# Two fetches of v earlier in a hybrid decoder layer, and two attention lanes that advance at every second step

## The chip, the cores and the metric

The kernel runs on one core of a Trainium2 chip. The metric is device time in microseconds of one execution; lower is better. TensorE (PE) does the matmuls, VectorE (DVE) and ScalarE (ACT) the elementwise work, GpSimd (POOL) a few small operations and part of the DMA issues, SyncE (SP) most of the DMA issues. Each engine works through its own queue of instructions in order.

## The reference

One layer on 256 tokens of width 2048, in float32. A normalised input is multiplied by one wide weight `w_in`, whose columns feed two mixers: chunked gated linear attention (GLA, branch a) and differential attention (branch b). Each mixer's output is normalised per head and gated, multiplied by its branch weight, and both are merged under sigmoid gates, multiplied by `w_out`, normalised and added to x.

```python
h = rmsnorm(x, pre_norm_g[l])
proj = h @ w_in[l]
(a_q, a_k, a_v, a_g, a_lr, b_q, b_k, b_v, b_g, m_a, m_b) = jnp.split(proj, offsets, axis=-1)
gk = jax.nn.log_sigmoid((a_lr @ gla_gk_w2[l] + gla_gk_b[l]).astype(jnp.float32)) / GATE_LOGIT_NORMALIZER
o_a = gla_chunked(a_q..., a_k..., a_v..., gk...)
o_a = rmsnorm(o_a, gla_norm_g[l]).reshape(B, S, GLA_VAL_DIM) * jax.nn.silu(a_g)
y_a = o_a @ w_branch_a[l]
o_b = diff_attention(b_q..., b_k..., b_v..., lam)
o_b = rmsnorm(o_b, diff_norm_g[l]) * (1.0 - lam_init)
o_b = o_b.reshape(B, S, DIFF_VAL_DIM) * jax.nn.silu(b_g)
y_b = o_b @ w_branch_b[l]
merged = jax.nn.sigmoid(m_a) * y_a + jax.nn.sigmoid(m_b) * y_b
x = x + rmsnorm(merged @ w_out[l], post_norm_g[l])
```

## The kernel before

**Products.** A float32 weight tile comes from HBM (`raw`, three buffers, loaded by SP at L308) and is split into two parts of reduced format: `hi` by ACT (L357) and the rest `lo` by DVE (L358), three buffers each. The stationary or moving operand (`xs` for the input, `oah`/`oal` for branch a's output, `obh`/`obl` for branch b's) is split in the same way, and each product is hi times hi, hi times lo, lo times hi. A weight tile has two halves; `take` splits three halves ahead of their use (AHEAD = 3). PE's matmuls for all of these stand at L552, in `mm`.

**Stages.** First the projection for v, k, q and the gates, with the blocks of `w_in` combined to save products; then the gates of branch a (`ag0` to `ag3`), m02, the last heads' q and k (`diff_heads(3)`, tiles `dq` and `dk` in column tiles of 128), m03; then `y00` to `y03` (branch a times its weight), the mixed steps of the branch (`branch_steps`: the rest of y03, parts of y10 and y11, and the products of the combined set `ys0`, whose weights are built in `part_e`, `part_b` and `part_f`), the late steps, and `w_out`.

**Tasks beside the main line.** GLA and differential attention run as generators in the list `tasks`. `pump(n)` advances the first n by one step after a piece of the main line; `pump_eager` advances, halfway through a column tile, those of the first two that last said "go". What a step issues is put in after the main line's matmuls before it. The tasks that matter here:

- `gla_scores(hf)` makes the scores of half the GLA heads (matmuls of `xq` and `xk`), hf 0 and then 1, and marks `scores0`, `scores1` when done.
- `gla_out` multiplies the scores by v. v was stored to HBM early on, in four parts (one per head) with a high and a low half each. `bring(n)` fetches part n into two tiles `vback` (512 KB each) with two DMAs on POOL's queue (L183, `fetch`). `weigh(n)` does nine matmuls of 512 columns on them (`product`, L525), two squares on ACT, the power for the norm on POOL (`rsqrt`, L459, tile `gssq`), and the gating on DVE (L1031). `turn_heads` transposes the result (L1037) into `oah`/`oal`.
- `diff_lane(0)` and `diff_lane(1)` work through the eight pairs of heads of branch b. Lane 0 starts at `scores1`, lane 1 when the fourth `weigh` is issued ("weighed"). Each fetches its q and k with small DMAs on SP's queue (`place`, L1066, into `q2`, `kh` and `kl`, after a memset of half of `kl` on POOL, L1079), makes scores (L1111 to L1117), turns them (L1142), multiplies them by v (`weighted`, L1153 to L1155; its own norm has a power on POOL, tile `de`), writes the gated head into `ogb` (L1166 on DVE), and at last turns the pair (`turned_out`, four transposes at L1172) into `obh` (ACT) and `obl` (DVE, L603).

**Buffers.** `vback`, `q2`, `kh`, `kl`, `gp`, the fetched q and k of GLA and `xs` all come from the pool `u` with 18 slots; a tile takes a free slot and its first writer waits for the slot's last reader.

The bodies that the change touches, of `gla_out` and of the branch's loop:

```python
        for n in range(7):
            if n < 4:
                weigh(n)
            if n < 2:
                bring(n + 2)
...
    for step in branch_steps():
        next(parts if step[0] in ("part", "ys0") else plain)
        if step == ("part", "ys0", 7, 1):
            merged(0, whole[0])
        pump(LANES if len(tasks) > 1 else 1)
```

LANES is 3. The branch has 26 steps in the order `.p.p.p.p.pp.pp.pp.p.p.p..p`, a dot being a step of y03, y10 or y11 (12 matmuls) and p one of ys0 (6 matmuls).

Of the kernel before, what the change touches and what calls it, by code (L numbers as in the profile page):

```python
# [24 lines left out]
LANES = 3  # L25
# [92 lines left out]
def half_set_steps(name):  # L118

    steps = []  # L120
    for prod in LATE:
        r = {1: 0, 2: 2}.get(prod)
        steps += [("part", name, prod, h) if r is None else (name, r, h) for h in range(2)]
    return steps


def branch_steps():

    plain = [("y03", r, h) for r in (2, 3) for h in range(2)]
    plain += [(f"y1{g}", r, h) for g in range(2) for r in range(2) for h in range(2)]  # L130
    parts = half_set_steps("ys0")
    return [(plain, parts)[n == "p"].pop(0) for n in BRANCH_ORDER]
# [11 lines left out]
def hybrid_kernel(ctx: ExitStack, tc, xt, xn, preg, postg, w, w2, gkb, glag, lamv, diffg, ident_d, causal_d, lmask_d, out):  # L144
# [18 lines left out]
    def u2(shape, name, dtype=F32):  # L163
        count[0] += 1
        return pools[1].tile(shape, dtype, tag="u2", name=f"{name}_{count[0]}")

    def sm(shape, name, dtype=F32, bufs=2):
        count[0] += 1
        return pools[0].tile(shape, dtype, tag=name, name=f"{name}_{count[0]}", bufs=bufs)
# [11 lines left out]
    def fetch(d, name, make, queue=pool):  # L181
        t = make(list(d.shape), name, d.dtype)
        tc.keep_in_program_order(queue.dma_start(t, d))  # L183
        return t

    def ps(tag):
        count[0] += 1
        return psum.tile([P, 512], F32, tag=tag, name=f"{tag}_{count[0]}")
# [269 lines left out]
    def rsqrt(dst, src):  # L458
        pool.tensor_tensor(out=dst, in0=src, in1=neg_half[:, : src.free_size()], op=ALU.pow)  # L459
# [41 lines left out]
    tasks = []  # L501
    ts, heads, m0 = {}, {}, []
    DONE = object()
    done = set()
# [4 lines left out]
    def advance(some):  # L509
        with tc.issue_after(latest[0]):  # L510
            for task in some:
                r = next(task, DONE)
                (eager.add if r == "go" else eager.discard)(task)
                if r is DONE:
                    tasks.remove(task)

    def pump(n=1):
        advance(tasks[:n])
# [4 lines left out]
    def product(out, pairs, first, last, **kw):  # L523
        for n, (lhs, rhs) in enumerate(pairs):
            i = pe.matmul(out, lhs, rhs, start=first and n == 0, stop=last and n == len(pairs) - 1, **kw)  # L525
        return i.ins
# [74 lines left out]
    def split_out(bank, hi, lo, gain):  # L601
        act.activation(hi, bank, AF.Copy, scale=gain)
        dve.scalar_tensor_tensor(out=lo, in0=bank, scalar=gain, in1=f32(hi), op0=ALU.mult, op1=ALU.subtract)  # L603
# [401 lines left out]
    def gla_out():  # L1005
        back = {}

        def bring(n):
            back[n] = [fetch(d, "vback", u) for d in vspill[n]]

        def weigh(n):
            hf, h = n // 2, n % 2
            if h == 0:
                for i in (2 * hf, 2 * hf + 1):
                    oah[i], oal[i] = u2([P, 2, 2, S], "oah", F32R), u2([P, 2, 2, S], "oal", F32R)
            (ah, al), (xh_, xl_) = att[hf], back.pop(n)
            banks = [ps("bg"), ps("bg")]
            trio = lambda i, b: ((ah[:, i, h, :], xh_[:, b, :]), (ah[:, i, h, :], xl_[:, b, :]), (al[:, i, h, :], xh_[:, b, :]))
            product(banks[0], trio(0, 0), True, True)
            product(banks[1], trio(2, 0), True, False)  # L1020
            product(banks[1], trio(1, 1), False, True)
            ssq = sm([P, 2], "gssq")
            junk = sm([P, 512], "junk", BF16, bufs=1)
            for b in range(2):
                act.activation(junk, banks[b], AF.Square, accum_out=ssq[:, b : b + 1])
            dve.scalar_tensor_tensor(out=ssq, in0=ssq, scalar=1.0 / 512.0, in1=gla_eps, op0=ALU.mult, op1=ALU.add)
            rsqrt(ssq, ssq)
            dve.tensor_tensor(out=ssq, in0=ssq, in1=half_rstd, op=ALU.mult)
            o = gates[n]
            for b in range(2):  # L1030
                dve.scalar_tensor_tensor(out=o[:, b, :], in0=banks[b], scalar=ssq[:, b : b + 1], in1=o[:, b, :], op0=ALU.mult, op1=ALU.mult)  # L1031

        def turn_heads(hf, j):
            bank = ps("bg")
            for h in range(2):
                for b in range(2):
                    pe.transpose(bank[:, P * (2 * h + b) : P * (2 * h + b) + P], gates[2 * hf + h][:, b, P * j : P * j + P], ident)  # L1037
            i = 2 * hf + j // 2
            hi = oah[i][:, j % 2].rearrange("p h t -> p (h t)")
            lo = oal[i][:, j % 2].rearrange("p h t -> p (h t)")  # L1040
            split_out(bank, hi, lo, glag_s[:, j : j + 1])

        while "scores0" not in done:
            yield
        bring(0)
        bring(1)
        yield
        while "scores1" not in done or len(gates) < 4:
            yield
        for n in range(7):  # L1050
            if n < 4:
                weigh(n)
            if n < 2:
                bring(n + 2)
            if n == 3:
                done.add("weighed")
            if n > 2:
                for j in range(2):
                    turn_heads((n - 3) // 2, 2 * ((n - 3) % 2) + j)
            yield "go"  # L1060
        done.add("out")

    obh, obl, ob_f32, ob_sums, values = [], [], [], {}, {}
# [175 lines left out]

    gates = []  # L1240
    tasks.append(gla_out())
    tasks.extend(diff_lane(n) for n in range(2))

# [110 lines left out]
    def merged(g, banks):  # L1354
        for b in range(2):
            t, src = gb[g][:, b, :], banks[b]
            if g < 2:
                src = ycell(b, g)
                dve.tensor_tensor(out=src, in0=banks[b], in1=src, op=ALU.add if 512 * g == BRANCH_COLS[0] else ALU.subtract)
            dve.scalar_tensor_tensor(out=t, in0=t, scalar=1.0, in1=src, op0=ALU.add, op1=ALU.mult)  # L1360
            dve.tensor_tensor(out=t, in0=t, in1=parts_a[g][:, b, :], op=ALU.add)
        tasks.append(turn(g))
# [152 lines left out]
    yc.extend(u([P, 1024], "yc") for _ in range(2))  # L1515
    parts, plain = half_set("ys0", b_ops, ob_sums, ycell, BRANCH_COLS), branch_plain(banks)
    pinned[0] = True
    for step in branch_steps():
        next(parts if step[0] in ("part", "ys0") else plain)
        if step == ("part", "ys0", 7, 1):  # L1520
            merged(0, whole[0])
        pump(LANES if len(tasks) > 1 else 1)
    pinned[0] = False
    for gen in (parts, plain):
        assert next(gen, DONE) is DONE
# [137 lines left out]
```

## Time and profile before

| what | us |
|---|---|
| time, three runs | 1095.33, 1095.60, 1097.95 (median 1095.6) |
| the profiled execution's own time | 1098.33 |
| its span, first to last instruction | 1096.5 |
| PE busy | 1081.7 |
| DVE busy | 931.6 |
| ACT busy | 721.3 |
| POOL busy | 154.2 |
| bytes read and written in HBM | 260.98 MB and 26.21 MB |

A line of the profile names an engine, a line of the kernel, an operation and the tiles `out<-in`, without their buffer numbers. "Busy" is time in which an engine executes; a busy PE can still run at a lower clock, which the column PEclk gives. The chain of work that ended last goes back from the last instruction to what released each step. In a timeline, what stands in brackets is the idle time ahead of an instruction on its engine and what ended it. Queue q0 is that of POOL's DMAs, q1 that of SP's.

### The profile page before, as it was taken

The numbers are of one execution on the slowest core, as the hardware profiler recorded it, in microseconds if no ns is written. First come the engines' busy times: TensorE is split into PE (matmuls) and PEld (weight loads), VectorE is DVE, ScalarE is ACT, GpSimd is POOL, SyncE is SP. The second block draws the span as 40 slices with busy tenths as digits, with TensorE's granted clock in tenths as the row PEclk, the third lists the DMA queues.
The fourth block names the chain that finished last, engine by engine and source line by source line (L and its number), as shares of the span: only waits on it lengthen the run. The fifth ranks groups of instructions, "written<-read, shape, count | busy, mean of one in ns | idle before, by whom it ended". The sixth has DMA issues, their size and how long they took to land.

```text
span 1096.5 us, 15366 instructions
## 1 busy us (share of the span) xinstructions
PE 1081.7 (99%) x5441; PEld 927.8 (85%) x5441; DVE 931.6 (85%) x1295; ACT 721.3 (66%) x1047; POOL 154.2 (14%) x229
## 2 busy tenths in 40 slices
PE   9999999999999999999999999989999999999997
PEld 8999888888888888888888888878888887888886
DVE  7787977979979899798999799866778878889886
ACT  7886766666766767677676465555777766566662
POOL 0211111121121221212111100021011012100000
PEclk9999999999999999999999999998999999999999
DMA  9889879798797997979879656598898899978752
GB/s 355 291 290 336 220 269 293 221 345 222 266 265 221 362 228 285 289 201 346 237 241 262 218 182 225 169 333 253 265 277 273 278 298 309 321 258 254 267 181 107
DMA packets 64941, 288.21 MB, mean 263 GB/s; under 512 B 8480, under 2 KB 11552, under 8 KB 46944
## 3 DMA queue, kind: packets, MB, share of 16 engines
q1 hardware_dynamic: 39520, 183.72, 47.9%
q0 software_dynamic: 24768, 102.77, 34.5%
q8 instruction: 43, 0.70, 0.3%
q10 hardware_dynamic: 576, 0.73, 0.2%
q14 instruction: 34, 0.28, 0.1%
HBM read 260.98 MB, written 26.21 MB: 262 GB/s over the span
## 4 chain that ended last, share of the span: by engine, by line
PE 93%; issue 3%; DMA 2%; DVE 1%; POOL 1%; ACT 0%; SPq 0%; POOLq 0%; ACTq 0%
PE mm L552 57%; PE bg L552 27%; PE mm L540 2%; PE bg L540 2%; PE mm L525 1%; DMA vback<-vl 1%; PE bg L977 1%; DMA part_e<-in_w_dram 1%; PE bg L525 1%; PE bg L444 0%; PE bg L1142 0%; PE bg L1116 0%; PE bg L1343 0%; PE bg L1037 0%; DVE lo L358 0%
## 5 line engine op out<-in xcount | busy, mean ns | idle before, releaser
L357 ACT ACTIVATE hi<-raw 128x1024 fp32r<-128x1024 f32 (+3 forms) x253 | 259.3, 1031 | 185.8 <-PE bg L552 92.3
L358 DVE TENSOR_TENSOR lo<-raw,hi 128x1024 fp32r<-128x1024 f32 (+3 forms) x255 | 300.8, 1184 | 61.7 <-ACT hi L357 58.8
L552 PE MATMUL mm<-hi,xs 128*128 128x512 f32 (+1 forms) x808 | 204.2, 385 | 0.0
L552 PEld LDWEIGHTS mm<-hi,xs 128*128 128x128 f32 x808 | 149.8, 188 | 24.8
L552 PE MATMUL bg<-xs,hi 128*128 128x512 f32 x640 | 164.8, 389 | 0.0
L358 DVE TENSOR_TENSOR lo<-a,hi 128x1024 fp32r<-128x1024 f32 x120 | 144.7, 1220 | 22.1 <-ACT hi L357 21.3
L357 ACT ACTIVATE hi<-a 128x1024 fp32r<-128x1024 f32 x120 | 127.1, 1060 | 45.2 <-PE mm L552 28.5
L552 PEld LDWEIGHTS bg<-xs,hi 128*128 128x128 f32 x640 | 120.3, 188 | 23.4
L552 PE MATMUL mm<-lo,xs 128*128 128x512 f32 (+1 forms) x404 | 112.8, 383 | 0.0
L552 PEld LDWEIGHTS bg<-xs,lo 128*128 128x128 f32 x640 | 87.3, 190 | 6.2
L552 PE MATMUL bg<-xs,lo 128*128 128x256 f32 x640 | 89.2, 282 | 0.0
L552 PEld LDWEIGHTS mm<-lo,xs 128*128 128x128 f32 x404 | 75.7, 188 | 13.6
L358 DVE TENSOR_TENSOR lo<-b,hi 128x1024 fp32r<-128x1024 f32 x60 | 72.4, 1221 | 6.5 <-ACT hi L357 5.0
L357 ACT ACTIVATE hi<-b 128x1024 fp32r<-128x1024 f32 x60 | 63.4, 1061 | 16.6 <-PE mm L552 14.6
L552 PE MATMUL mm<-hi,oah 128*128 128x512 f32 x128 | 50.9, 398 | 0.2 <-ACT ob_copy L1190 0.2
L552 PE MATMUL mm<-hi,oal 128*128 128x512 f32 x128 | 50.0, 391 | 0.0
L251 POOL DMA_DIRECT2D b<-in_w_dram x30 | 26.0, 868 | 136.7 <-DVE a L260 120.3
L1128 ACT ACTIVATE prob<-prob,mx,score_scale 128x128 f32<-128x128 f32 x64 | 34.2, 538 | 7.6 <-DVE mx L1123 7.3
L552 PE MATMUL mm<-hi,obh 128*128 128x512 f32 x96 | 37.7, 392 | 0.0
L552 PE MATMUL mm<-hi,obl 128*128 128x512 f32 x96 | 37.4, 390 | 0.0
L357 ACT ACTIVATE hi<-c 128x1024 fp32r<-128x1024 f32 x30 | 31.7, 1059 | 7.8 <-PE mm L552 5.8
L260 DVE TENSOR_TENSOR a<-a,b 128x1024 f32<-128x1024 f32 x30 | 36.3, 1220 | 0.3
(417 smaller groups left out, 2071.3 us busy)
## 6 DMA issues: line engine op xcount, KB each, us to landing
raw<-in_w_dram SPq DMA_DIRECT2D x110, 1024.0 KB, 6.7
a<-in_w_dram POOLq DMA_DIRECT2D x30, 512.0 KB, 12.0
c<-in_w_dram SPq DMA_DIRECT2D x30, 512.0 KB, 8.7
b<-in_w_dram POOLq DMA_DIRECT2D x30, 512.0 KB, 8.1
a<-in_w_dram POOLq DMA_DIRECT2D x13, 1024.0 KB, 8.0
b<-in_w_dram POOLq DMA_DIRECT2D x13, 1024.0 KB, 8.5
raw<-in_w_dram SPq DMA_DIRECT2D x14, 832.0 KB, 7.1
gr<-gr POOLq DMA_DIRECT2D x8, 512.0 KB, 7.4
```

The source lines that it names most:

```text
L251: pool.dma_start(chain[s, name, i][:, c], block(s, 1, i)[:, c], accum_op=ALU.add)
L260: dve.tensor_tensor(out=a, in0=a, in1=chain[s, "b", i][:, c] if second else raws[s, i, h], op=ALU.add)
L357: act.activation(hi_t[:, a:b], r[:, a:b], AF.Copy)
L358: dve.tensor_tensor(out=lo_t[:, a:b], in0=r[:, a:b], in1=f32(hi_t[:, a:b]), op=ALU.subtract)
L525: i = pe.matmul(out, lhs, rhs, start=first and n == 0, stop=last and n == len(pairs) - 1, **kw)
L540: i = pe.matmul(banks[g][b][:, :n], a[part][:, P * b : P * b + P], w[:, n * g : n * g + n], start=first, stop=last)
L552: i = pe.matmul(*args, **kw)
L977: pe.matmul(o, xk[:, P * c : P * c + P], xq.rearrange("p (b c t) -> p b c t", b=2, c=4)[:, :, c, :], start=i == 0, stop=i == 1)
L1128: act.activation(prob[m][:, lo:up], prob[m][:, lo:up], AF.Exp, scale=score_scale[:, b : b + 1], bias=mx[:, i : i + 1], accum_out=z[:, i : ...
```

## The change

The third part of v is fetched as soon as `scores1` is there, ahead of the first `weigh`; the fourth after the first `weigh` and no longer after the second. After the second `weigh` the task says None in place of "go". In the branch's mixed steps, as long as a lane is unfinished, tasks advance only at every second step (the odd ones, counted from 0).

```diff
         bring(0)
         bring(1)
         yield
-        while "scores1" not in done or len(gates) < 4:
+        while "scores1" not in done:
+            yield
+        bring(2)
+        while len(gates) < 4:
             yield
         for n in range(7):
             if n < 4:
                 weigh(n)
-            if n < 2:
-                bring(n + 2)
+            if n == 0:
+                bring(3)
             if n == 3:
                 done.add("weighed")
             if n > 2:
                 for j in range(2):
                     turn_heads((n - 3) // 2, 2 * ((n - 3) % 2) + j)
-            yield "go"
+            yield None if n == 1 else "go"
...
-    for step in branch_steps():
+    for n, step in enumerate(branch_steps()):
         next(parts if step[0] in ("part", "ys0") else plain)
         if step == ("part", "ys0", 7, 1):
             merged(0, whole[0])
-        pump(LANES if len(tasks) > 1 else 1)
+        if n % 2 or {"lane0", "lane1"} <= done:
+            pump(LANES if len(tasks) > 1 else 1)
```

The fetches stand on POOL's queue, where the third and fourth part of v are vh_950/vl_952 and vh_1197/vl_1199; the `dh` and `dl` rows are stores of the heads' q. Before, from the end of `gla_scores(1)` on:

```order
L178 DMA dh_6527<-dh_6524 128x512
L178 DMA dl_6529<-dq_6399 128x512
L459 TENSOR_TENSOR gssq_6601<-gssq_6601,neg_half 128x2
L183 DMA vback_6610<-vh_950 128x1024
L183 DMA vback_6612<-vl_952 128x1024
L1079 MEMSET kl_6616 64x512 x2
L459 TENSOR_TENSOR gssq_6659<-gssq_6659,neg_half 128x2
L183 DMA vback_6668<-vh_1197 128x1024
L183 DMA vback_6670<-vl_1199 128x1024
```

And now:

```order
L178 DMA dl_6529<-dq_6399 128x512
L183 DMA vback_6586<-vh_950 128x1024
L183 DMA vback_6588<-vl_952 128x1024
L459 TENSOR_TENSOR gssq_6605<-gssq_6605,neg_half 128x2
L183 DMA vback_6614<-vh_1197 128x1024
L183 DMA vback_6616<-vl_1199 128x1024
L1082 MEMSET kl_6620 64x512 x2
L459 TENSOR_TENSOR gssq_6663<-gssq_6663,neg_half 128x2
```

The third part has moved ahead of the first `weigh`'s power, the fourth ahead of lane 0's memset and the second `weigh`'s power. PE's queue in this stage is the same row for row, and so are DVE's, ACT's and SP's apart from tile numbers.

In the branch PE's queue changes. Before, after the last matmul of y03's first step of the branch (`lo_8437`), with the turn of a finished pair (`ogb`), the product with v (`dv`) and the turn of scores (`prob`), all of one lane, and ys0's first step (`obh`, `obl`):

```order
L552 MATMUL mm_8409<-lo_8437,oah_6695 128x512
L1172 MATMUL mm_8590<-ident,ogb_8452 128x128 x4
L1153 MATMUL bg_8600<-dv_8224,prob_796_8383 128x128
L1154 MATMUL bg_8600<-dv_8224,prob_796_8383 128x128
L1155 MATMUL bg_8600<-dv_8224,prob_796_8383 128x128
L1142 MATMUL bg_8615<-ident,prob_815_8478 128x128 x3
L552 MATMUL bg_8620<-hi_8504,obh_7340 128x512
L552 MATMUL bg_8620<-hi_8504,obl_7341 128x512
...
L552 MATMUL bg_8620<-lo_8505,obh_7340 128x512 x2
```

And now:

```order
L552 MATMUL mm_8409<-lo_8437,oah_6695 128x512
L552 MATMUL bg_8590<-hi_8504,obh_7340 128x512
L552 MATMUL bg_8590<-hi_8504,obl_7341 128x512
...
L552 MATMUL bg_8590<-lo_8505,obh_7340 128x512 x2
L1175 MATMUL mm_8601<-ident,ogb_8452 128x128 x4
L1156 MATMUL bg_8611<-dv_8224,prob_796_8383 128x128
L1157 MATMUL bg_8611<-dv_8224,prob_796_8383 128x128
L1158 MATMUL bg_8611<-dv_8224,prob_796_8383 128x128
L1145 MATMUL bg_8626<-ident,prob_815_8478 128x128 x3
```

The lane's four pieces have moved behind ys0's first step. The lane's next two pieces (the product with v of its second head, and its last turn) move back in the same way, by two and by three steps.

On DVE, a little later in the branch, the lane's second head (`de`, `ogb`) and its last `obl` stand between the splits (`lo`) and the additions to `part_e`. Before:

```order
L1162 SCALAR_TENSOR_TENSOR de_8639<-dssq_8635,de_8639 128x2
L1164 TENSOR_TENSOR de_8639<-de_8639,half_rstd 128x2
L1166 SCALAR_TENSOR_TENSOR ogb_8599<-bg_8631,de_8639,ub_8226 128x128 x2
L358 TENSOR_TENSOR lo_8647<-part_e_8430,hi_8646 128x1024
L603 SCALAR_TENSOR_TENSOR obl_8596<-mm_8663,diffg_s,obh_8595 128x512
L294 TENSOR_TENSOR part_e_8430<-part_e_8430,part_b_8500 128x1024
L358 TENSOR_TENSOR lo_8671<-raw_8572,hi_8670 128x1024
L358 TENSOR_TENSOR lo_8685<-part_e_8433,hi_8684 128x1024
L294 TENSOR_TENSOR part_e_8433<-part_e_8433,part_b_8502 128x1024
L358 TENSOR_TENSOR lo_8703<-raw_8682,hi_8702 128x1024
```

And now:

```order
L358 TENSOR_TENSOR lo_8632<-part_e_8430,hi_8631 128x1024
L294 TENSOR_TENSOR part_e_8430<-part_e_8430,part_b_8500 128x1024
L358 TENSOR_TENSOR lo_8649<-raw_8572,hi_8648 128x1024
L1165 SCALAR_TENSOR_TENSOR de_8668<-dssq_8664,de_8668 128x2
L1167 TENSOR_TENSOR de_8668<-de_8668,half_rstd 128x2
L1169 SCALAR_TENSOR_TENSOR ogb_8610<-bg_8660,de_8668,ub_8226 128x128 x2
L358 TENSOR_TENSOR lo_8678<-part_e_8433,hi_8677 128x1024
L294 TENSOR_TENSOR part_e_8433<-part_e_8433,part_b_8502 128x1024
L358 TENSOR_TENSOR lo_8696<-raw_8675,hi_8695 128x1024
L603 SCALAR_TENSOR_TENSOR obl_8607<-mm_8705,diffg_s,obh_8606 128x512
```

The last `obl` now ends this stretch, behind both additions; the second PSUM bank of y10 is the one that this `obl` reads, so y10's third matmul waits for it.

## The prediction

> **What bounds the kernel now.** I read the page first, then PE's waits over the whole run, then the chain and the rows around the two longest of them.
>
> From the page, its first row of busy times and the chain's shares by engine:
>
> ```profile
> PE 1081.7 (99%) x5441; PEld 927.8 (85%) x5441; DVE 931.6 (85%) x1295; ACT 721.3 (66%) x1047; POOL 154.2 (14%) x229
> ...
> PE 93%; issue 3%; DMA 2%; DVE 1%; POOL 1%; ACT 0%; SPq 0%; POOLq 0%; ACTq 0%
> ```
>
> TensorE is the bound nearly everywhere. No matmul is added or removed, so the change can win only where PE waits or runs slowly. The view of PE's waits (who waited for whom: us in total, times, longest) has as its first, second and fourth row:
>
> ```profile
> PE bg L525 <- DMA vback<-vh: 3.8, 1, 3.8
> PE mm L1172 <- DVE ogb L1166: 2.1, 1, 2.1
> ...
> PE bg L525 <- DMA vback<-vl: 1.3, 1, 1.3
> ```
>
> L525 is `product`, called by `weigh`; L1172 is `turned_out` in a lane. The edits touch exactly these two places. PE's timeline at the first:
>
> ```profile
> 734.99 0.39 PE L552 MATMUL mm<-xs,hi 128*128 128x512 f32 x1
> 739.14 0.56 PE L525 MATMUL bg<-vback,ath 128*128 128x512 f32 x1 [3.76 <-DMA vback<-vh]
> 741.05 0.79 PE L525 MATMUL bg<-vback,ath 128*128 128x512 f32 x1 [1.35 <-DMA vback<-vl]
> ```
>
> PE is done at 734.99 + 0.39 = 735.38, stands 3.76 us until the high half of v's third part lands and 1.35 us more for its low half: 5.11 us. What follows runs slowly (the chain; start, length):
>
> ```profile
> 741.05 3.78 PE bg L525 x8
> 744.83 3.48 PE mm L552 x16
> 748.31 2.07 PE bg L525 x9
> ...
> 751.26 2.79 PE mm L552 x16
> ```
>
> The stage at 748.31 is the fourth `weigh`, the same nine products in 2.07 us; 16 matmuls that took 3.48 after the wait take 2.79 later. The granted clock says why (windows: stretch, length, PE busy, PEclk, DMA share, GB/s):
>
> ```profile
> 738.00:740.00 2.00, 0.56 (x1) 0.84 1.43 289
> ...
> 742.00:744.00 2.00, 2.00 (x6) 0.50 1.17 234
> ...
> 746.00:748.00 2.00, 2.00 (x13) 0.95 1.05 292
> ...
> 906.00:908.00 2.00, 0.60 (x4) 1.00 0.61 117
> ```
>
> The 3.76 us cost half the clock until about 746; the 2.07 us at 907 cost none.
>
> **The change part by part.**
>
> **1. Parts three and four of v asked for sooner.** POOL's timeline and the age of one store:
>
> ```profile
> 722.77 0.55 POOL L178 DMA_DIRECT2D dl<-dq  x1 [0.25 <-DVE dq L779]
> 728.97 0.72 POOL L459 TENSOR_TENSOR gssq<-gssq,neg_half 128x2 f32<-128x2 f32 x1 [5.65 <-DVE gssq L1026]
> 729.65 0.59 POOL L183 DMA_DIRECT2D vback<-vh  x1
> 730.23 0.55 POOL L183 DMA_DIRECT2D vback<-vl  x1
> ```
>
> ```profile
> dl<-dq POOLq DMA_DIRECT2D x1, 256.0 KB, 3.5
> ```
>
> Before, the third part's two DMAs stand behind the first `weigh`'s power, which waits for DVE until 728.97, and go out at 729.65 and 730.23. Now they stand right behind the store `dl`: 722.77 + 0.55 = 723.3, and some 0.6 later, 6.3 us sooner. POOL does nothing else from 723.3 to 728.97, so the move delays no POOL work. The fourth part takes the third's old place at 729.65. Their slots held tensors of the finished scores, so no new wait for a buffer comes with it; lane 0 gets other, equally free slots. SP's queue is the same row for row.
>
> Do they land in time? The third is wanted at 735.38, the fourth one stage and one half later: 735.38 + 2.07 + 2.79 = 740.24. Issued at 729.65 and 730.23 the third landed where PE's waits end, 739.1 and 741.0: 9.5 and 10.8 us. By that price it lands at 732.8 and 734.7, in time by 0.7. By another, bytes in a stretch of the DMA view (packets, MB, share):
>
> ```profile
> q1 hardware_dynamic: 163, 1.20, 54.1%
> q0 software_dynamic: 362, 1.22, 52.7%
> ...
> q1 hardware_dynamic: 242, 0.97, 96.6%
> ...
> q0 software_dynamic: 229, 0.82, 85.6%
> q1 hardware_dynamic: 181, 0.31, 40.3%
> ```
>
> The first pair is 720 to 726, the middle row 726.4 to 729.6, the last pair 734 to 738; q0 is POOL's queue, q1 SP's. Against SP's load q0 moved 1.22 MB in 6 us or 0.82 in 4, about 204 GB/s. In the middle stretch it moved nothing: dl had landed at 722.77 + 3.5 = 726.3, and the next fetch was not asked for. That hole is what the change fills. Two fetches of 512 KB are 1.05 MB, 5.1 us at 204 GB/s: the third part is in at 731.4, the fourth, queued at once behind it, at 736.5. At worst the fourth takes as long behind the third as the third took before: 734.7 + 10.8 = 745.5, a wait of 5.3 us. I take the measured rate, and no wait.
>
> What is won: from 735.38 to the fourth `weigh` at 748.31 are 12.93 us; at full clock one stage and one half are 4.86. **8.1 us**, of which 5.1 are standing and 3.0 the slow clock.
>
> Here a page bears on it: the Trainium skill, "TensorE: Matmul & The Clock Gate", Part 1, has the clock halved after an idle window of about 3.4 us that runs freely, so that the same wait may or may not cost it. The trace agrees with a drop at 3.76 us and none at 2.07; by the rule edit 1 is worth between 5.1 and 8.1 from one execution to the next, by the traced one alone 8.1.
>
> **2. "Spaced".** After the second `weigh` the task gives None instead of "go". The next advance is then a plain `pump` anyway, since it stands at the end of a column tile; PE's order in this stage is the same row for row. Zero.
>
> **3. Lanes advance at every second step of the branch.** PE there, with the price of one ys0 step from the chain:
>
> ```profile
> 904.94 0.38 PE L1172 MATMUL mm<-ident,ogb 128*128 128x128 f32 x2
> 907.39 0.59 PE L1172 MATMUL mm<-ident,ogb 128*128 128x128 f32 x2 [2.07 <-DVE ogb L1166]
> ...
> 908.98 1.38 PE bg L552 x6
> ```
>
> Now one ys0 step stands ahead of the four transposes and fills 1.38 of the 2.07 us; its hi and lo come three halves ahead, so it is ready. What may be late next is the lane's last `obl`: it now stands behind both additions to part_e on DVE, and the second bank of y10, which begins here,
>
> ```profile
> 923.91 0.39 PE L552 MATMUL mm<-hi,obh 128*128 128x512 f32 x1
> ```
>
> now waits for it (before, that bank waited for PE alone). DVE's groups from 907 to 923 (count | busy us, mean ns | idle before):
>
> ```profile
> L358 DVE TENSOR_TENSOR lo<-raw,hi 128x1024 fp32r<-128x1024 f32 x4 | 4.9, 1220 | 0.0
> ...
> L294 DVE TENSOR_TENSOR part_e<-part_e,part_b 128x1024 f32<-128x1024 f32 x2 | 2.4, 1220 | 0.0
> L1166 DVE SCALAR_TENSOR_TENSOR ogb<-bg,de,ub 128x128 f32<-128x128 f32 x6 | 1.8, 347 | 0.1
> L603 DVE SCALAR_TENSOR_TENSOR obl<-mm,diffg_s,obh 128x512 fp32r<-128x512 f32 x2 | 1.5, 748 | 0.0
> ...
> L1164 DVE TENSOR_TENSOR de<-de,half_rstd 128x2 f32<-128x2 f32 x2 | 0.3, 162 | 1.6 <-POOL de L459 1.6
> ```
>
> In the new order DVE has from the ogb at 907.6 to that obl: eight passes of 1.22 (9.8), four ogb (1.4), two obl (1.5), two de with their POOL wait (1.9), and three more tiny ones at the same 0.16 (0.5): 15.1 us, so 922.7. PE comes to the second bank at 923.91 - 1.38 + two matmuls, about 923.0. The margin is 0.3; DVE idles between these by some tenths to 2 us. So this edit is worth 1.38 at best (2.07 if the wait goes whole) and -0.6 at worst. I take the middle of 1.38 and 0, **0.7 us**. Both lanes still end before y10 begins, so `settle` pumps nothing. The lanes' rsqrt on POOL come a few us later and part_f's accumulations with them; these are wanted only in the last ys0 products, far behind, and cost nothing.
>
> **Sum.** The profiled execution took 1098.33: its span of 1096.5 and 1.8 around it. 1098.33 - 8.1 - 0.7 = **1089.5**. It lies 2.7 above the median of 1095.6, and the three times are 1095.33, 1095.60 and 1097.95: a spread of 2.6, near the 3.0 of the slow clock. I read it so that the median's execution stood still but kept its clock: 1095.6 - 5.1 - 0.7 = 1089.8. Both meet.
>
> **The rivals.**
>
> - *Every execution pays the slow clock*, and the 2.7 is the profile's own: 1095.6 - 8.1 - 0.7 = 1086.8. For it: the wait alone halves the clock in the one trace. Against: the spread.
> - *The fourth part inherits the wait.* It lands at the worst price, 745.5, PE stands 5.3 us and pays the clock again: edit 1 gives nothing, 1095.6 - 0.7 = 1094.9. For it: before, the two fetches together took from 729.65 to 741.0. Against: that began with an empty queue; the rate behind it was 204 GB/s. Half way, a wait of 2.5 without the clock: 1092.3.
> - *The weight loads starve: slower.* Both fetches now run against SP's queue, which holds one load of w and ten small copies for the lanes. In the last pair above q0 took 0.82 MB and q1 only 0.31. The load to watch is the one SP issues at 740.89:
>
> ```profile
> raw<-in_w_dram SPq DMA_DIRECT2D x1, 1024.0 KB, 11.0
> ...
> 761.41 1.06 ACT L357 ACTIVATE hi<-raw 128x1024 fp32r<-128x1024 f32 x1 [1.97 <-PE mm L552]
> ```
>
> It lands at 751.9 and its first split, by the order of the splits, is the one at 761.41, held by PE, not by the load. With PE 8.1 sooner it is wanted at 753.3, and three halves (3 x 2.79, 8.4 us) are split ahead. The bytes ahead of it are the same ones, and the hole is filled. To end above 1095.6 PE would have to stand more than 8.8 us: the load would have to land 18.6 us late (1.4 + 8.4 + 8.8), near 770.5. From there every us is a us lost; three more give 1099.
>
> Behind this stands a rule that speaks against the change: the Trainium skill, "DMA: Bandwidth & Descriptors", Queues, rings and completion order, has each DMA engine take turns between queues packet by packet, so whatever POOL is given early is taken from SP. The first pair (1.22 to 1.20 MB) agrees; the last (0.82 to 0.31) does not share by bytes. By it SP's load would lose at most the time of the third part's 1.05 MB, 5.1 us at 204 GB/s, less than the 9.8 us it has.
>
> **How the numbers follow.** Forecast (1089.5, within about 1.5) 0.58; slow clock in all (1086.8) 0.22; fourth part half late (1092.3) 0.08, fully late (1094.9) 0.08; starved loads (1099) 0.04. Range 1086 to 1092.6: it leaves out the last two cases and takes in edit 3's bounds (+1.3, -1.4). A measurement of this kernel can tell about 0.3%, 3.3 us, from no change: faster is below 1092.3. Forecast, slow clock and half of the half-late case with what of it lies below give 0.85; within 0.3% 0.11; slower 0.04.
>
> **What would show it.** Right: POOL's two vback rows near 723.5, L525 without a wait, PEclk at 1.00 from 734 to 748, the fourth `weigh` near 740; at the branch PE's wait for ogb below 0.7. Wrong: a wait of L525 on vback at the fourth `weigh`; ACT waiting for a raw load near 753; a wait of L552 for obl where y10 begins; a median near 1087.

## The result, and the profile after

The changed kernel takes 1090.35 us (median of 6 executions, 1089.00 to 1091.06) where the kernel before, run beside it, takes 1096.8 (median of 6). The ratio is 0.9937, 95% interval 0.9921 to 0.9953: 6.9 us faster, between 5.1 and 8.7. The profiled execution took 1090.66, with a span of 1088.8; that of before took 1098.33, with 1096.5. The forecast was 1089.5 with a range of 1086 to 1092.6. Two executions among the experiments below, one of third_only and one of both_early, ran at a mean granted clock of 0.654 and took 1542 us; they are left out of the medians (with them 1096.57 and 1089.24).

The page of after, busy time of PE, and the shares of the chain that ended last:

```profile
PE 1079.6 (99%) x5441; PEld 926.3 (85%) x5441; DVE 931.2 (86%) x1295; ACT 720.4 (66%) x1047; POOL 154.4 (14%) x229
...
PE 96%; DMA 1%; issue 1%; DVE 1%; ACT 0%; POOL 0%; POOLq 0%; ACTq 0%
```

PE's share of the chain rose from 93% to 96%, and its busy time fell by 2.1 us although it does the same matmuls: that fits the work which ran at half the clock before, from 741 to 746.5, and does so no longer. PE's waits (us in total, times, longest; L1175 is now the line of the lane's last transposes):

```profile
PE bg L525 <- DMA vback<-vl: 1.0, 1, 1.0
...
PE mm L1175 <- DVE ogb L1169: 0.6, 1, 0.6
```

The wait of 3.8 for the high half is gone, that for ogb went from 2.1 to 0.6. But L525 still waits 1.0 for a low half. PE's timeline says for which, and the windows (stretch, length, PE, PEld, DVE, ACT, POOL busy, PEclk, DMA share, GB/s) what its clock did:

```profile
735.84 0.83 PE L525 MATMUL bg<-vback,ath 128*128 128x512 f32 x2
...
740.89 0.39 PE L525 MATMUL bg<-vback,ath 128*128 128x512 f32 x1
742.33 0.50 PE L525 MATMUL bg<-vback,ath 128*128 128x512 f32 x1 [1.05 <-DMA vback<-vl]
```

```profile
738.00:740.00 2.00, 2.00 (x11) 1.65 (x10) 1.23 (x4) 1.32 (x3) 0.59 (x1) 1.00 1.22 287
...
742.00:744.00 2.00, 1.68 (x7) 1.42 (x8) 1.47 (x2) 0.69 (x2) 0.55 (x1) 1.00 0.77 244
...
746.00:748.00 2.00, 2.00 (x15) 1.76 (x14) 1.72 (x4) 0.38 (x1) 0.21 (x1) 1.00 0.86 298
```

The third `weigh` runs at 735.84 without a wait and the granted clock stays at 1.00. The wait has moved to the fourth: its second product stands 1.05 us. From PE's last product before the third `weigh` (it ends at 736.01) to the fourth at 740.89 are 4.88 us, where before had 12.93 and full clock was reckoned at 4.86. POOL's timeline, and the chain there:

```profile
723.92 0.55 POOL L183 DMA_DIRECT2D vback<-vh  x1
724.65 0.55 POOL L183 DMA_DIRECT2D vback<-vl  x1 [0.18 <-issue]
...
730.26 0.58 POOL L183 DMA_DIRECT2D vback<-vh  x1
730.84 0.54 POOL L183 DMA_DIRECT2D vback<-vl  x1
```

```profile
730.84 11.44 DMA vback<-vl
742.28 0.04 issue
742.33 2.12 PE bg L525 x8
```

The fetches are issued where the prediction put them. The fourth part's low half lands 11.4 us after its issue, at 742.28, not at 736.5. The third part's low half also takes 11.5 us, from 724.65 to 736.12: it is there just as PE comes for it.

At the branch, PE's first and second pair of a lane's transposes, then DVE's last `obl` and the product that begins y10's second bank:

```profile
900.38 0.38 PE L1175 MATMUL mm<-ident,ogb 128*128 128x128 f32 x2
901.39 0.59 PE L1175 MATMUL mm<-ident,ogb 128*128 128x128 f32 x2 [0.62 <-DVE ogb L1169]
```

```profile
915.05 0.74 DVE L603 SCALAR_TENSOR_TENSOR obl<-mm,diffg_s,obh 128x512 fp32r<-128x512 f32 x1
```

```profile
916.72 0.39 PE L552 MATMUL mm<-hi,obh 128*128 128x512 f32 x1
```

The last `obl` is done at 915.79, the bank is wanted at 916.72. The wait that the prediction feared isn't there, by 0.9 us.

### The profile page after: what moved, and what is told of

It reads as the page before. It is cut to its first block, busy times and chain, and to the rows that moved or that the text cites. A ratio compares the mean times of both kernels' runs of the same rounds, so it can differ in the third digit from the quotient of the medians.

```text
span 1088.8 us, 15368 instructions
## 1 busy us (share of the span) xinstructions
PE 1079.6 (99%) x5441; PEld 926.3 (85%) x5441; DVE 931.2 (86%) x1295; ACT 720.4 (66%) x1047; POOL 154.4 (14%) x229
## 4 chain that ended last, share of the span: by engine, by line
PE 96%; DMA 1%; issue 1%; DVE 1%; ACT 0%; POOL 0%; POOLq 0%; ACTq 0%
PE mm L552 59%; PE bg L552 27%; PE mm L540 2%; PE bg L540 2%; DMA vback<-vl 1%; PE mm L525 1%; PE bg L977 1%; PE bg L1145 0%; PE bg L444 0%; PE bg L1119 0%; PE bg L1120 0%; PE bg L1346 0%; PE bg L1037 0%; PE mm L1175 0%; PE bg L1157 0%
```

## The experiments

Twelve runs in three groups, each with the kernel before beside it; its medians were 1097.1, 1098.03 and 1097.71, so ratios compare better than times. Every run has one trace. **First the two edits apart**, and the fourth part's place.

The fetches alone (edit 3 undone):

```diff
-        if n % 2 or {"lane0", "lane1"} <= done:
-            pump(LANES if len(tasks) > 1 else 1)
+        pump(LANES if len(tasks) > 1 else 1)
```

> Only the fetches moved (edits 1 and 2); lanes advance at every branch step as before. Theory: edit 3 was worth about 1.4 us (PE's wait for ogb fell from 2.07 to 0.62), so this is 1.4 above the changed kernel's 1090.35: near 1091.8, 5.0 below before, with the 2.07 us wait back at the lane's last transposes and no wait for the third part, 1.0 for the fourth. Rival: edit 3 gave its gain back later (a wait for the last obl, or other work pushed back): then this is no slower than 1090.4. The prediction's 0.7 would give 1091.1.

Measured: 1092.34, ratio 0.9959 [0.9947, 0.9971], that is 4.5 us below before (3.2 to 5.8). Its first and fourth waits of PE:

```profile
PE mm L1175 <- DVE ogb L1169: 1.8, 1, 1.8
...
PE bg L525 <- DMA vback<-vl: 0.9, 1, 0.9
```

The lanes alone (edits 1 and 2 undone):

> Only edit 3. Theory: 1.4 below before, so 1095.4 where before has 1096.8; the waits of 3.76 and 1.35 us for the third part stay, and the granted clock falls to about 0.50 behind them in some executions only, so that the times lie in two groups some 3 us apart. Rival (every execution pays the slow clock): one group, spread below 2 us.

Measured: 1095.82, ratio 0.9989 [0.9980, 0.9998], 1.2 below before (0.2 to 2.2). The twelve times run from 1094.70 to 1097.82 in one group, without the two groups that were expected (the rival expected one group, but with a spread below 2 us); the mean granted clock was 0.995 to 0.998. Waits:

```profile
PE bg L525 <- DVE dk L772: 2.7, 1, 2.7
...
PE bg L525 <- DMA vback<-vl: 1.0, 1, 1.0
PE mm L1172 <- DVE ogb L1166: 0.6, 1, 0.6
```

(The 2.7 us are the wait for the third part's high half; the view names `dk`, which had long been done, since the high half landed at 738.42 and the product began at 738.56.) So both edits win, the second by little more than the noise, and 4.5 and 1.2 make 5.7, inside the whole change's interval. Edit 2 alone wasn't run: with it and without it the program is the same, row for row on all five engines.

The third part alone (`if n == 1` in place of `if n == 0` ahead of `bring(3)`):

> The third part asked for early, the fourth after the second weigh as before. It is issued near 736 and wanted near 740.9. Theory (POOL's queue moves its bytes one after the other; a megabyte takes about 6.2 us once it flows, 736.1 to 742.3 in the changed kernel): it lands near 744, a wait of about 3 us, the clock in doubt: 2 to 5 us slower than the changed kernel, 1092.4 to 1095.4. Rival (a fetch takes about 11.4 us from its issue, whatever stands ahead): it lands near 747.5, a wait of 6 to 7 us that halves the clock: 8 us or more slower, 1098. Second rival (the fourth's move bought nothing): the changed kernel's time.

Measured: 1096.04, ratio 0.9989 [0.9974, 1.0003].

```profile
742.76 0.47 PE L525 MATMUL bg<-vback,ath 128*128 128x512 f32 x1 [2.46 <-DMA vback<-vh]
745.53 0.80 PE L525 MATMUL bg<-vback,ath 128*128 128x512 f32 x1 [2.30 <-DMA vback<-vl]
```

```profile
746.00:748.00 2.00, 2.00 (x6) 1.54 (x6) 0.00 (x0) 0.69 (x2) 0.00 (x0) 0.50 1.12 358
```

The landing, at 745.5, lies between the two theories, and so does the price: by the ratios it is 5.7 us slower than the changed kernel, where the theory had 2 to 5 and the rival 8 or more. PE stands 4.8 us one stage later, and the clock falls. The ratio is that of the lanes alone, so what is left is edit 3's 1.2. The third part's move is worth nothing without the fourth's.

Both parts right behind the first scores (`bring(3)` moved up to `bring(2)`):

> Third and fourth part both asked for right behind the first scores, ahead of the first weigh: the fourth is issued near 725.5 instead of 730.5. Theory (the queue's bytes go one after the other at the rate that SP's queue leaves): the fourth still lands near 742 and its wait of 1.0 us stays; same time within 0.5 us as the changed kernel. Rival (11.4 us from the issue): the fourth lands near 737, no wait, 1.0 us faster, 1089.3. Third case: the two parts share the queue, the third lands late (after 736) and PE stands there instead: slower by 1 to 4 us.

Measured: 1089.15, ratio 0.9930 [0.9917, 0.9944]. The third and the fourth `weigh`, and the eight fetches' time to landing (min, median, max):

```profile
735.76 0.62 PE L525 MATMUL bg<-vback,ath 128*128 128x512 f32 x2
...
740.58 0.63 PE L525 MATMUL bg<-vback,ath 128*128 128x512 f32 x2
```

```profile
DMA to landing us min/median/max: 6.8/9.3/13.0
```

The longest, 13.0, is the fourth part's low half: issued at 725.64, it lands at 738.64, 1.9 us before it is wanted, and the third part is not later for it (734.53, where after had 736.12). No wait is left here. The theory of bytes one after the other at a fixed rate (a landing near 742) falls, and so does a fixed 11.4 us from the issue.

**Then what holds the landings.** Lane 0 is started after the third `weigh`, so that its small copies on SP's queue come later:

```diff
+            if n == 2:
+                done.add("third")
...
-        while ("scores1", "weighed")[n] not in done:
+        while ("third", "weighed")[n] not in done:
```

> The changed kernel, with lane 0 started after the third weigh instead of the first scores, so that its small copies on SP's queue come some 11 us later; the two fetches keep their places. Theory (the 11.4 us of each low half are lost to SP's queue, its 1 MB load of w and the lane's copies): the third part's low half lands in 9 us or less and the fourth's near 739.5, so that PE's wait of 1.0 us for it goes; the median may be worse for other reasons, since the lane is late from there on. Rival (POOL's own queue sets the pace): landings at 11 us as before, the wait stays.

Measured: 1090.21, ratio 0.9928 [0.9916, 0.9941]. The DMA view: the fourth part's two issues (KB each, us to landing), and the queues from 732 to 736 (packets, MB, share), first of after:

```profile
vback<-vh POOLq DMA_DIRECT2D x1, 512.0 KB, 9.3
vback<-vl POOLq DMA_DIRECT2D x1, 512.0 KB, 11.4
...
q1 hardware_dynamic: 368, 0.61, 75.4%
q0 software_dynamic: 99, 0.37, 44.4%
```

and of this kernel:

```profile
vback<-vh POOLq DMA_DIRECT2D x1, 512.0 KB, 4.0
vback<-vl POOLq DMA_DIRECT2D x1, 512.0 KB, 5.2
...
q0 software_dynamic: 289, 1.03, 76.1%
q1 hardware_dynamic: 61, 0.49, 31.0%
```

Without the copies POOL's queue (q0) moves 1.03 MB in the same 4 us instead of 0.37, and the low halves land in 8.4 and 5.2 us instead of 11.5 and 11.4. Only lane 0's start was moved, so its copies on SP's queue are what stretches the fetches. In halves the 4 us look so: from 732 to 734 SP moved 0.37 MB and POOL 0.12 in the changed kernel, nothing and 0.73 here; from 734 to 736 SP moved 0.25 MB in 154 packets beside POOL's 0.25, and here 0.49 MB in 60 packets beside POOL's 0.29. PE waits for no part of v here. The time isn't told apart from the changed kernel's (ratios 0.9937 and 0.9932 in its two runs).

**The slow clock by itself.** First a second trace of before:

> The kernel before once more, for a second trace of it. What the third part's wait costs in its trace: 12.93 us from PE's last product to the fourth weigh in the first one. Theory: that one was at the dear end, since its landings took 9.4 and 10.8 us while those of only_lanes, the same code at this place, took 8.3 and 9.6 and cost 11.4 us in all; here between 11 and 13 us, with a granted clock of 0.50 behind the wait. Rival: a trace without the slow clock (below 10.5 us).

```profile
738.69 0.47 PE L525 MATMUL bg<-vback,ath 128*128 128x512 f32 x1 [1.99 <-DMA vback<-vh]
741.54 0.72 PE L525 MATMUL bg<-vback,ath 128*128 128x512 f32 x1 [2.38 <-DMA vback<-vl]
```

```profile
742.00:744.00 2.00, 2.00 (x6) 1.55 (x5) 0.00 (x0) 0.69 (x2) 0.00 (x0) 0.50 1.32 297
```

Measured: 1097.99, ratio 1.0002 [0.9990, 1.0014]. PE's last product ends at 736.70 and the fourth `weigh` starts at 747.86: 11.16 us, a loss of 6.3 against 4.86, again with the clock at half. The third part took 7.6 and 9.9 us here. Next, products that fill the waits of before, so that PE doesn't stand; ten of them ahead of the third `weigh`:

```diff
+            if n == 2:
+                for _ in range(10):
+                    pe.matmul(banks[0], ah[:, 0, h, :], att[0][0][:, 0:2].rearrange("p i h t -> p (i h t)"), start=True, stop=True)
             product(banks[0], trio(0, 0), True, True)
```

> The kernel before, with ten more products of 128x512 (0.22 to 0.24 us each by the rows of others, so about 2.3 us) right ahead of the third weigh's first product, into the bank that it then overwrites; nothing else differs. They run inside the wait for the third part (3.76 us in the trace of before, 2.73 in that of only_lanes), so they cost nothing, and PE no longer stands more than some 1.5 us at a stretch. This prices the slow clock by itself. Theory A (nearly every execution of before pays the slow clock, as the mean granted clock of 0.994 to 0.998 in all 23 of its runs says): the clock stays at 1.00 and the time falls by about 3.0 us, ratio 0.9973, clock 0.999. Theory B (the prediction's reading: the median execution stood still but kept its clock): the median doesn't move, ratio 1.000. Third case: extra work that outlasts the wait where the part lands early, up to 0.5 us slower.

Measured: 1097.63, ratio 0.9996 [0.9986, 1.0005].

```profile
735.97 2.45 PE L1021 MATMUL bg<-ath,ath 128*128 128x512 f32 x10
738.26 0.45 PE L525 MATMUL bg<-vback,ath 128*128 128x512 f32 x1
740.84 0.80 PE L525 MATMUL bg<-vback,ath 128*128 128x512 f32 x1 [2.13 <-DMA vback<-vl]
...
906.73 0.59 PE L1175 MATMUL mm<-ident,ogb 128*128 128x128 f32 x2 [2.42 <-DVE ogb L1169]
```

```profile
742.00:744.00 2.00, 2.00 (x7) 1.52 (x6) 0.62 (x1) 1.21 (x3) 0.00 (x0) 0.50 1.32 285
908.00:910.00 2.00, 2.00 (x8) 1.62 (x7) 1.20 (x4) 1.16 (x6) 0.69 (x1) 0.51 1.00 408
```

The clock fell all the same, behind a wait of 2.13 us, and a second time behind ogb's 2.42. Of the twelve executions five had a mean clock of 0.999 (1095.3 to 1096.9) and seven 0.996 to 0.998 (1097.4 to 1099.2). That looks like a price of 2 us or so, but an execution in which the third part lands early has both a shorter wait and less reason for the clock to fall, so it doesn't tell cause from company. Hence ten more products, behind the first real one, into the other bank:

> The kernel before, with ten products ahead of the third weigh's first product and ten more behind it (into the other bank, which is then overwritten), so that PE runs through both waits for the third part: 2.3 us each, where the waits were 2.0 to 3.8 and 1.0 to 2.4 us. This finishes what warm left open: there 5 of 12 runs kept the clock (0.999) at 1095.3 to 1096.9 and 7 did not (0.996 to 0.998) at 1097.4 to 1099.2. Theory A (the slow clock costs 2.5 to 3 us in nearly every run of before): all runs at 0.998 or 0.999, near 1096, that is 2 us below before, since the second ten outlast the second wait by up to 1 us in some executions. Theory B (the clock's drop costs nothing in the median): 1098, as before, or above it by what the added products outlast the wait.

Measured: 1098.56, ratio 1.0003 [0.9992, 1.0013]; eight of twelve executions at 0.998 or 0.999, yet only three below 1096.4. The eight have a median of 1097.87, no lower than before's 1097.71.

```profile
737.83 2.45 PE L1021 MATMUL bg<-ath,ath 128*128 128x512 f32 x10
740.12 0.39 PE L1024 MATMUL bg<-vback,ath 128*128 128x512 f32 x1
740.35 2.43 PE L1026 MATMUL bg<-ath,ath 128*128 128x512 f32 x10
...
748.70 0.50 PE L525 MATMUL bg<-vback,ath 128*128 128x512 f32 x1 [1.11 <-DMA vback<-vl]
```

In this trace the clock was 1.00 from 732 to 760, and over the twelve executions the time didn't fall. PE's last product ended at 738.00 and the fourth `weigh` started at 747.19, 9.19 us, 4.3 above 4.86. To that come 1.11 us of a new wait, for the fourth part: 5.4 lost, where before_again lost 6.3 with the slow clock. The added products outlast the landing (741.85) by 0.75 us, and the fourth part, asked for as late as in before, lands at 748.65. So against before_again's trace the kept clock saves 0.9 us here: the wait for the next part takes the rest. That isn't the whole account. In the traces of before, before_again and only_lanes the fourth part had landed 2.4, 1.2 and 2.3 us before the fourth `weigh` started (at 745.89, 746.71 and 744.83), so there that much of the slow clock's cost lay over no such wait. Why the median didn't fall all the same stays open. This one trace has time lost elsewhere too: PE reached the third `weigh` at 738.00, 1.3 to 2.6 us later than in those three, and it waits 2.0 us for ogb.

**Last, the better versions side by side.** Both parts early; the same with lanes at every third step (`n % 3 == 2` in place of `n % 2`), which had a run of its own first:

> Both parts early, and lanes advance at every third branch step instead of every second, so that one more half (2.79 us) stands ahead of the four transposes that still wait 0.75 us for ogb. Theory: that wait goes, 0.7 below both_early's 1089.24: 1088.5. Rival (what the prediction feared of edit 3: the lane's last output is late where y10 begins): a wait of L552 for obl or for the last transposes of 1 to 3 us there, 1090 to 1092.

Measured: 1089.92, ratio 0.9922 [0.9909, 0.9935]. The time misses the 1088.5 of the theory; by the ratios it is 0.0008 below both_early. PE waits neither for ogb nor for `obl`, but for `lo` three times, 0.8 us in all, and once 1.2 us for `hi` at L540:

```profile
902.72 0.60 PE L1174 MATMUL mm<-ident,ogb 128*128 128x128 f32 x4
```

> The changed kernel once more, beside the two better candidates. Theory: 1090.4 as before, ratio 0.9935; PE's wait for the fourth part's low half between 0.5 and 1.5 us in the trace, clock 0.998 to 1.000.

> Both parts early, lanes at every second step. Theory: the fourth part's wait of 1.0 us is gone, so 1.0 below after_again on the same chip: near 1089.3, ratio 0.9926. Rival (the difference of the first round was the chip's): no difference from after_again beyond 0.3 us.

> Both parts early, lanes at every third step. Theory: 0.6 below both_early_again, since ogb's wait of 0.6 to 0.75 us goes: near 1088.7. Rival (what the profile of its first run hints at, with waits of 0.2 to 0.6 us for lo): the wait only turns into others, same as both_early_again within 0.3 us.

| kernel, same group | median us | ratio to before |
|---|---|---|
| changed kernel | 1090.81 | 0.9932 [0.9919, 0.9946] |
| both parts early | 1089.53 | 0.9921 [0.9907, 0.9934] |
| both early, every third step | 1088.88 | 0.9915 [0.9901, 0.9928] |

Both parts early is 1.3 us below the changed kernel in this group, where 1.0 was expected, but the two intervals overlap. Nor does the wait account for it here: the changed kernel's second trace waits only 0.4 us for the fourth part, below the expected 0.5 to 1.5. That the wait goes is shown, in both traces of both_early; what that is worth in time is not settled. Every third step removes the wait for ogb in both of its traces; by the ratios it gains another 0.0008 and 0.0006 over every second step, well inside the intervals: not settled either.

## Why the prediction was right, and where not

The time was 0.85 us above the forecast and well inside the range, faster as said. By its steps:

- **Edit 1, where the fetches go out: right.** 723.92 and 730.26 for the high halves, and no wait at the third `weigh`.
- **Edit 1, when they land: wrong.** The failed step is "I take the measured rate, and no wait". The 204 GB/s came from two stretches in which POOL's queue did well. In one, 720 to 726, SP's queue carried a large load (1.20 MB in 163 packets); in the other, 734 to 738, it already carried lane 0's copies, but few packets of them (181). The stretch between them, right behind the third part's issue at 729.65, was not looked at; in before, from 728 to 732, the queues are

```profile
q1 hardware_dynamic: 474, 0.95, 99.5%
q0 software_dynamic: 2, 0.01, 0.7%
```

So beside SP's load and copies the fetch moved next to nothing in the first 2.3 us after its issue. In the changed kernel from 732 to 736 SP sent 368 packets, and q0 got 0.37 MB in the 4 us where 0.82 had been counted on: 736.12 instead of 731.4 for the third part, 742.28 instead of 736.5 for the fourth. The second price in the text, taken from the third part's own fetch, gave 734.7, nearer and still early. The rival "the fourth part inherits the wait" happened at a fifth of its full size: 1.05 us of 5.3. held_copies shows the cause: lane 0's copies on SP's queue.
- **The slow clock: half right.** That it goes is right (1.00 throughout). That "the median's execution stood still but kept its clock" is not borne out: in the 63 executions of before that ran beside the experiments the mean clock was 0.994 to 0.998, and 0.998 to 1.000 in the changed kernel's twelve; the second trace of before, at 0.998, has the clock at half too. The profiled execution was slow at least in part because its third part landed late (9.4 and 10.8 us, against 7.6 and 9.9 in the second trace, which lost 6.3 us instead of 8.1), not because it alone paid the clock. The trace's 8.1 was the dear end: the two other traces with this code lost 6.3 (before_again) and 6.5 (only_lanes). Less the 1.05 that stays, that is 5.3 to 5.4; only_parts measured 4.5 (3.2 to 5.8). The prediction's 5.1 by the median fits it by luck, through two errors that nearly cancel: it left out the clock, and it left out the fourth part's wait. The base helped as well: the forecast is 6.1 below a median of 1095.6, measured were 6.9 below 1096.8.
- **The rule of the Trainium skill, "TensorE: Matmul & The Clock Gate", Part 1**, an idle window of about 3.4 us, doesn't hold here as the least wait that costs the clock: it fell behind single waits of 2.13 and 2.42 us (warm), and not behind 2.07 (before). The Trainium skill's 3.4 us do show in how long the clock stays down (below).
- **Edit 2: right**, nothing.
- **Edit 3: right in kind, perhaps too small.** 0.7 was the middle of 0 and 1.38; the runs give 1.2 (0.2 to 2.2, which holds 0.7 too). The wait for ogb is 2.07, 0.89, 1.84, 2.42 and 2.0 in five traces without the edit, and 0.75 at most in those with it. The feared wait for `obl` was worked out nearly right: from the end of the first ogb to the last `obl` 15.1 us were reckoned and 14.2 passed (901.59 to 915.79), and the margin was 0.9 instead of 0.3.
- **Starved loads: didn't happen.** ACT's splits of loads from 750 to 765 still wait for PE alone. The load that SP issues at 724.5 took 10.4 us against 9.2 before, but that is no more than it varies (9.2 and 7.9 in the two traces of before, 10.4 and 9.1 in the changed kernel's). SP's loss is in the copies: those of q that it issues from 723.2 to 731 took 13.0 and 13.1 us in the median (`dh` and `dl`), against 7.6 to 8.3 in the two traces of before, and PE waited for none of them. That fits the turns by packets between the queues (the Trainium skill, "DMA: Bandwidth & Descriptors", Queues, rings and completion order): what POOL is given, SP loses, and in held_copies POOL gains what SP doesn't ask for.

## What to carry to other kernels

A prefetch must be priced against what the other queues will carry in its new place, over the whole stretch from its issue to its landing, not against the best rate that was seen elsewhere. Ask for it as early as its buffer allows, and look for the next transfer in the row, which inherits the wait (the third part alone won nothing). Before a stall's price is taken from one trace, look at how the waits and the mean clock vary over executions. And a slow clock is not always a cost of its own, since the next wait can lie over it: keeping PE busy through the stall kept the clock in eight of twelve executions and won nothing in the median.

## What was not expected of the hardware

- The granted clock halved behind single waits of PE of 2.1 to 2.4 us; other waits of 2.0 to 2.1 (before, warm_through) left it at 1.00.
- It stayed down for one length or twice that. Over the windows of 2 us, what PEclk lacks from 1.00, divided by the half, gives the time: in warm 0.69, 0.50 and 0.95 make 3.4 us, behind ogb 0.51 and 0.64 make 3.4; in before_again 0.91, 0.50 and 0.73 make 3.4; in the first trace of before 0.84, three times 0.50 and 0.95 make 6.8. At half speed that is 1.7 or 3.4 us of work lost, if PE has work all that time.
- Small copies on SP's queue hurt a fetch on POOL's more than their bytes say: in 734 to 736 POOL moved 0.25 MB beside 0.25 MB of SP's in 154 packets (the changed kernel), and 0.29 MB beside 0.49 MB of SP's in 60 packets (held_copies). In before, from 728 to 732, 474 packets of SP's left POOL's queue 0.01 MB.
- Fetches queued behind one another slowed none ahead of them: with the fourth part asked for 5 us sooner, the third landed no later (734.5 against 736.1). Its low half took 9.9 to 10.6 us in the four traces with both parts early, and 10.8 to 11.6 in the four others that ask for it at the same place (the changed kernel's two, only_parts, third_only).
